# Third and fourth part of a paired feed-forward block exchanged (6, 6, 4, 6), with later activation, rounding and one later product

## The chip, the cores and the metric

The kernel runs on one core of a Trainium2 chip. The metric is the device time of one execution in microseconds (us); the kernel before takes 2537.56 us, the median of 3 runs (2536.77 to 2540.05). The core has a matrix engine (TensorE, PE in the profile), a vector engine (VectorE, DVE), an activation engine (ScalarE, ACT), a general engine (GpSimd, POOL) and SyncE (SP), which here only issues transfers. Each works through a queue of its own in order.

## The reference

The reference is one step of a streaming encoder of two layers, for 512 prompt frames and 64 sample frames that share one set of weights. All is float32, with a model width of 1024. Cut to what matters:

```python
def swiglu(x, w_gu, w_down):
    gate, up = jnp.split(x @ w_gu, 2, axis=-1)      # w_gu: 1024 x 5632
    return (jax.nn.silu(gate) * up) @ w_down        # w_down: 2816 x 1024

for l in range(2):
    x = x + 0.5 * swiglu(rms_norm(x, ln_ffn1[l]), w_ffn1_gu[l], w_ffn1_down[l])
    x = x + mixer(rms_norm(x, ln_mix[l]))           # l=0: attention heads and a short convolution; l=1: state space
    x = x + cross_attend(rms_norm(x, ln_cross[l]), mem_k, mem_v, w_xq[l], w_xo[l])
    x = x + 0.5 * swiglu(rms_norm(x, ln_ffn2[l]), w_ffn2_gu[l], w_ffn2_down[l])
y = rms_norm(x, ln_final)
```

The outputs are y for both groups of frames and the new caches of the mixers and of the memory attention. Of the four feed-forward blocks (FFNs) the change touches three: the second of layer 0 and both of layer 1.

## The kernel before, in words

**Layout.** The 512 + 64 frames lie side by side as 576 columns, in two halves of 288; features lie on the 128 partitions. The state X is 8 tiles of 128 features, and the hidden layer of an FFN has 2816 features, 22 tiles. Every float32 product is made of three products of rounded operands: a weight is split into a rounded part `wh` (by ACT, `hi`, L148) and a rest `wl` (by DVE, `lo`, L154; in steps that are not paired L231), an input likewise into `xh` and `xl` (hidden tiles into `hh`, `hl`), and PE adds wh·xh, wh·xl and wl·xh.

**Pairs.** In the three FFNs of the list `LAYERS_S` the gate and up tile of one hidden tile (called gate/up pair gN here, N from 0 to 21), and each two output tiles f and f + 4 of the down projection (down pair d0 to d3), are computed together in the manner of Strassen and Winograd: seven products over half the rows and half the columns of the operands, in place of eight, with sums of weights and differences of inputs as operands (`eh`, `el` are rounded differences of the normed input; `qeh`, `qel` those of the hidden tiles). g2.3 is product k = 3 of gate/up pair 2. A gate/up product has 12 matmuls (4 tiles of 128 rows by 3 parts), a down product as many tiles as the hidden part has halved: 3 tiles and 9 matmuls for a part of 6 hidden tiles. The matmuls of all pair products stand in one line, L340.

**Banks.** A pair has three PSUM banks, called T, Y and W (`PLACE`): products 0, 3, 4 and 6 write T in turn, 1 and 5 write Y, 2 writes W. Pairs take two sets of banks alternately. After each product an epilogue reads the bank: `pair_epi` (L555) for gate/up, with the evictions L570 (ACT, `tb`), L572 (DVE, `ta` = T + tb), L578 (ACT, `tc`) and L600 (DVE, `tc` = T + tb), the multiplication by the norm's factor (L585), the silu (L588), and after the pair's last product the hidden tile (L618 to L620) and its differences `hk` (L624, or L627 to L629). Then `tail` asks ACT for their rounding and `rest` asks DVE for the rests. `down_epi` (L648) adds a product to X (L655).

**Order of products.** `pair_steps` (L316) gives product k of pair n the place 7n + at[k] from tables written by hand, sorts the products by place, and issues them as steps. `at` has entries of its own for the first two pairs, for the last pair and for d0. `defer(fn, n)` (L399) holds a request back for n further steps; `tick` counts them.

**Weights.** `run_steps` (L166) runs ahead of the product that PE is at: SP loads both tiles of a pair (L292, L293; at most three loads open, at most some eleven products ahead), POOL issues an accumulating transfer into the second buffer (L301), DVE makes the sum `ss` (L310) when the pair's product 2 is prepared, and POOL accumulates twice into the first buffer (L312, L314). Rounding by ACT and DVE is done a few products ahead of the matmuls.

**Parts.** The hidden tiles are worked in parts, `PARTS_S` = 6, 6, 6 and 4 tiles. After the gate/up pairs of a part, and the first one of the next, come the part's four down pairs; their products overlap the neighbours'. The last part's down projection is not paired ("direct"): for each of 8 output tiles, 3 matmuls per hidden tile and column half. For the first two FFNs that is `down` (matmuls in `proj`, L419; X at L727), for the last `down_two` and `down_final` with 320 and then 256 columns (matmuls L738, X at L743), followed by the final norm and its transposes (L2230, L2232). Columns of the down weights are laid out by `KORDER`, so that in a paired part the even hidden tiles come ahead of the odd ones.

Of the kernel before, what the change touches and what calls it, by code (L numbers as in the profile page):

```python
# [22 lines left out]
FF = 2816  # L23
NJ = 22
PARTS = ((0, 6), (6, 8), (14, 8))
PARTS_S = ((0, 6), (6, 6), (12, 6), (18, 4))
KORDER = [j0 + j for j0 in (0, 6, 12) for j in (0, 2, 4, 1, 3, 5)] + [18, 19, 20, 21]
LAYERS_S = ((2, 0), (1, 1), (2, 1))
PAIRED = (0, 4, 1, 5, 2, 6, 3, 7)
PAST = 256  # L30
# [55 lines left out]
class Kernel:  # L86
# [229 lines left out]
    def pair_steps(self, pairs):  # L316

        mm = self.nc.tensor.matmul  # L320
        todo = []
        for n, pr in enumerate(pairs):
            pr.banks = [self.banks[:, 3 * (n % 2) + b, :HF] for b in range(3)]
            at = {2: 0, 0: 3, 1: 4, 3: 6, 5: 8, 4: 9, 6: 12}
            if n < 2:
                at = ({0: 0, 1: 1, 2: 4, 3: 6, 5: 8, 4: 9, 6: 12}, {0: -5, 1: -4, 2: -2, 3: 0, 4: 3, 5: 4, 6: 7.5})[n]
            elif n == len(pairs) - 1:
                at = {0: 0, 2: 0.5, 3: 3, 1: 4, 4: 6, 5: 7, 6: 9}
            elif pr.f == 0:
                at = {0: 0, 2: 3, 1: 4, 3: 6, 5: 8, 4: 9, 6: 12}  # L330
            todo += [(7 * n + at[k], k, pr) for k in range(7)]

        def one(w, k, pr):
            out = pr.banks[PLACE[k]]
            xh, xl = pr.ops()[k]
            kn = pr.kw // 128
            for kk in range(kn):
                ws = slice(kk * 128, kk * 128 + 128)
                for pi, (ww, xx) in enumerate(((w[0], xh), (w[0], xl), (w[1], xh))):
                    mm(out, ww[:, ws], xx[:, kk], start=k < 3 and kk == 0 and pi == 0, stop=kk == kn - 1 and pi == 2,  # L340
                       skip_group_check=True)
            pr.epi(k, pr)

        for _, k, pr in sorted(todo, key=lambda t: t[0]):
            self.step(lambda w, k=k, pr=pr: one(w, k, pr), Part(pr, k))
# [204 lines left out]
    def ffn(self, gu, dn, gain_next, pairs=True, early=False):  # L550
# [1 line left out]
        V = nc.vector  # L552
        st = {}

        def pair_epi(k, pr, first, last, direct):  # L555

            T, Y, W = pr.banks
            tt = V.tensor_tensor
            jj = pr.jj
# [15 lines left out]
            elif k == 1:  # L575
                self.hi(pr.tb[:, two], Y)
            elif k == 3:
                self.hi(pr.tc[:, one], T)  # L578
                if first:
                    st["r"] = self.stats_tok(self.acc, self.ones, 1.0, ps=self.banks[:, 6:8])  # L580
                elif "R" not in st:
                    st["dg"] = self.diag(st["r"], "td")
            elif k == 5:
                def gate(c=slice(0, NT)):
                    tt(pr.ta[:, c], pr.ta[:, c], st["R"][:, c], op=ALU.mult)  # L585

                def silu():
                    nc.scalar.activation(pr.ta, pr.ta, AF.Silu)  # L588

                tt(pr.ta[:, two], Y, pr.tc[:, one], op=ALU.add)  # L590
                if first:
                    st["R"] = self.stats_bcast(None, dg=st.pop("dg"), ps=self.banks[:, 6:8])
                if last:
                    gate(two)
                    silu()
                else:
                    gate()
                    self.defer(silu, 1)
            elif k == 4:
                tt(pr.tc[:, two], T, pr.tb[:, two], op=ALU.add)  # L600
            else:
                qh, ql = st["qhh"], st["qhl"]
                kk = jj // 2
                hk = st["hk"]
                if direct or jj % 2:
                    h = self.tmp("td")
                else:
                    h = hk[:, 1:3].rearrange("p c n -> p (c n)")
                if last:
                    hh, hl = st["hh"][:, jj], st["hl"][:, jj]  # L610
                    for c, x in ((one, T), (two, pr.tc[:, two])):
                        tt(h[:, c], x, pr.ta[:, c], op=ALU.mult)
                        tt(h[:, c], h[:, c], st["R"][:, c], op=ALU.mult)
                        self.hi(hh[:, c], h[:, c])
                    for c in (one, two):
                        self.lo(hl[:, c], h[:, c], hh[:, c])
                    return
                tt(h[:, one], T, pr.ta[:, one], op=ALU.mult)  # L618
                tt(h[:, two], pr.tc[:, two], pr.ta[:, two], op=ALU.mult)
                tt(h, h, st["R"], op=ALU.mult)  # L620
                if direct:
                    parts = [(st["hh"][:, jj], st["hl"][:, jj], h)]
                elif jj % 2 == 0:
                    tt(hk[:, 0], hk[:, 1], hk[:, 2], op=ALU.subtract)  # L624
                    parts = [(qh[:, 0:2, kk], ql[:, 0:2, kk], hk[:, 0:2])]
                else:
                    tt(hk[:, 2], h[:, two], hk[:, 2], op=ALU.subtract)  # L627
                    V.scalar_tensor_tensor(hk[:, 1], hk[:, 2], -1.0, hk[:, 1], op0=ALU.mult, op1=ALU.subtract)
                    V.scalar_tensor_tensor(hk[:, 0], h[:, one], -1.0, hk[:, 1], op0=ALU.mult, op1=ALU.subtract)  # L629
                    parts = [(qh[:, 2:4, kk], ql[:, 2:4, kk], self.h2(h)),  # L630
                             (st["qeh"][:, :, kk], st["qel"][:, :, kk], hk[:, 1:3]),
                             (qh[:, 4, kk], ql[:, 4, kk], hk[:, 0])]

                def rest():
                    for oh, ol, x in parts:
                        self.lo(ol, x, oh)

                def tail():
                    for oh, ol, x in parts:
                        self.hi(oh, x)  # L640
                    self.defer(rest, 0 if first or jj == 5 else 1)

                if jj == 0 and not first:
                    st["held"] = tail
                else:
                    self.defer(tail, 0 if first or jj == 5 else 1)

        def down_epi(k, pr, last):  # L648

# [9 lines left out]
        ops = lambda: self.pair_ops(self.xh, self.xl, self.eh, self.el)  # L659
# [3 lines left out]

        def gate_up(j, jj, nj, direct):
            pr = Pair(gu[2 * j], gu[2 * j + 1],
                      lambda k, pr: pair_epi(k, pr, j == 0, direct and jj == nj - 1, direct), ops)
            pr.jj, pr.begun = jj, False
            seq.append(pr)

# [4 lines left out]

        parts = PARTS_S if pairs else PARTS
        for pi, (j0, nj) in enumerate(parts):
# [97 lines left out]
            for jj in range(0 if pairs else nj):  # L774
                j = j0 + jj
# [1581 lines left out]
def host_arrays(i):  # L2357
# [23 lines left out]
    for n in ("1", "2"):  # L2381
        out["gu" + n] = gu(f(f"w_ffn{n}_gu"))
        out["dn" + n] = np.stack([cols(w) for w in f(f"w_ffn{n}_down")])
        for l in range(2):
            if (int(n), l) in LAYERS_S:
                w = out["dn" + n][l].reshape(8, 128, NJ, 128)
                out["dn" + n][l] = w[:, :, KORDER].reshape(8, 128, NJ * 128)

# [84 lines left out]
```

## Time and profile before

| what | before |
|---|---|
| time, median of 3 runs | 2537.56 us |
| profiled execution | 2532.74 us |
| its span | 2531.0 us |
| mean granted TensorE clock | 0.989 |
| busy PE / DVE / ACT / POOL | 2445.7 / 1841.0 / 1154.5 / 619.1 us |
| paired FFNs, about | 917 to 1328, 1328 to 1733, 2116 to 2531 us |

The profile is one execution, with times from the start of its span. Rows of the timeline and of a tile or line give start, duration, engine, line, operation, output and inputs, shape, and in brackets how long the engine was idle ahead of it and what released it. A group's row gives count, then busy us and the mean in ns, then the idle time. Rows of the waits give the total, the number and the longest. The chain of waits, or chain that ended last, gives start, length, and what ran. The granted clock is a share of TensorE's full speed.

### The profile page before, as it was taken

The numbers are of one execution on the slowest core, as the hardware profiler recorded it, in microseconds if no ns is written. First come the engines' busy times: TensorE is split into PE (matmuls) and PEld (weight loads), VectorE is DVE, ScalarE is ACT, GpSimd is POOL, SyncE is SP. The second block draws the span as 40 slices with busy tenths as digits, with TensorE's granted clock in tenths as the row PEclk, the third lists the DMA queues.
The fourth block names the chain that finished last, engine by engine and source line by source line (L and its number), as shares of the span: only waits on it lengthen the run. The fifth ranks groups of instructions, "written<-read, shape, count | busy, mean of one in ns | idle before, by whom it ended". The sixth has DMA issues, their size and how long they took to land.

```text
span 2531.0 us, 46506 instructions
## 1 busy us (share of the span) xinstructions
PE 2445.7 (97%) x18175; PEld 2398.4 (95%) x18175; DVE 1841.0 (73%) x3350; ACT 1154.5 (46%) x2099; POOL 619.1 (24%) x775
## 2 busy tenths in 40 slices
PE   8999999999999999999989999999999999999997
PEld 8999999999899999999979999999999999999997
DVE  5645658667875588898888888876743468888885
ACT  5222222324664455445455454453443455554544
POOL 1576235202420012222202222212311001222221
PEclk9999999999999999999999999999999999999998
DMA  4365653321134355767736767665972235576771
GB/s 149 92 187 185 155 127 114 127 87 36 41 124 134 106 134 129 181 155 161 154 101 142 165 144 175 141 166 191 297 242 83 77 101 134 134 179 152 160 156 63
DMA packets 160091, 353.21 MB, mean 140 GB/s; under 512 B 21584, under 2 KB 64256, under 8 KB 159232
## 3 DMA queue, kind: packets, MB, share of 16 engines
q1 hardware_dynamic: 115808, 277.09, 34.1%
q0 software_dynamic: 44064, 73.16, 18.7%
q8 instruction: 143, 2.34, 0.4%
q14 instruction: 76, 0.62, 0.1%
HBM read 293.83 MB, written 31.97 MB: 129 GB/s over the span
## 4 chain that ended last, share of the span: by engine, by line
PE 63%; DVE 20%; ACT 6%; DMA 4%; issue 4%; POOL 3%; SPq 0%; DVEq 0%; ACTq 0%; POOLq 0%
PE banks L340 26%; PE banks L419 25%; DVE wl L154 3%; ACT wh L148 2%; PE banks L1988 2%; DVE wl L231 2%; PE banks L2264 2%; PE banks L1884 1%; DVE hl L154 1%; PE banks L1369 1%; PE banks L1337 1%; DMA b<-in_ssm_bw 1%; DVE td L620 1%; ACT hh L148 1%; DMA s5y<-yw 1%
## 5 line engine op out<-in xcount | busy, mean ns | idle before, releaser
L148 ACT ACTIVATE wh<-wraw 128x512 fp32r<-128x512 f32 (+3 forms) x639 | 441.6, 713 | 290.6 <-PE banks L340 104.6
L231 DVE TENSOR_TENSOR wl<-wraw,wh 128x1024 fp32r<-128x1024 f32 (+2 forms) x216 | 260.3, 1209 | 146.7 <-ACT wh L148 144.2
L340 PE MATMUL banks<-xh,wh 128*128 128x288 f32 x1056 | 314.1, 297 | 3.1 <-ACT wh L148 1.9
L340 PE MATMUL banks<-xh,wl 128*128 128x288 f32 x1056 | 314.0, 297 | 1.8 <-DVE wl L154 1.8
L340 PE MATMUL banks<-xl,wh 128*128 128x288 f32 x1056 | 314.0, 297 | 0.2 <-DVE xl L156 0.2
L154 DVE TENSOR_TENSOR wl<-wraw,wh 128x512 fp32r<-128x512 f32 (+1 forms) x408 | 259.3, 640 | 62.8 <-ACT wh L148 60.8
L419 PE MATMUL banks<-xh,wh 128*128 128x288 f32 x1232 | 268.6, 300 | 9.5 <-ACT wh L148 8.6
L419 PE MATMUL banks<-xh,wl 128*128 128x288 f32 x1232 | 266.4, 298 | 3.2 <-DVE wl L231 3.2
L419 PE MATMUL banks<-xl,wh 128*128 128x288 f32 x1232 | 266.0, 298 | 0.0
L340 PE MATMUL banks<-eh,wh 128*128 128x288 f32 x792 | 239.2, 302 | 26.9 <-DVE tc L600 14.5
L340 PE MATMUL banks<-el,wh 128*128 128x288 f32 x792 | 235.5, 297 | 0.0
L340 PE MATMUL banks<-eh,wl 128*128 128x288 f32 x792 | 235.4, 297 | 0.0
L314 POOL DMA_DIRECT2D wraw<-ss x102 | 89.4, 884 | 537.4 <-DVE ta L572 215.9
L419 PE MATMUL banks<-hh,wh 128*128 128x288 f32 x968 | 209.2, 298 | 4.6 <-ACT wh L148 2.0
L419 PE MATMUL banks<-hl,wh 128*128 128x288 f32 x968 | 208.5, 297 | 4.7 <-DVE hl L154 4.7
L419 PE MATMUL banks<-hh,wl 128*128 128x288 f32 x968 | 208.3, 297 | 3.4 <-DVE wl L231 3.2
L419 PEld LDWEIGHTS banks<-xh,wh 128*128 128x128 f32 x1232 | 200.0, 190 | 11.8 <-ACT wh L148 9.1
L340 PEld LDWEIGHTS banks<-xh,wh 128*128 128x128 f32 x1056 | 201.1, 190 | 3.8 <-ACT wh L148 2.3
L419 PEld LDWEIGHTS banks<-xh,wl 128*128 128x128 f32 x1232 | 200.4, 191 | 4.6 <-DVE wl L231 4.4
L340 PEld LDWEIGHTS banks<-xh,wl 128*128 128x128 f32 x1056 | 200.6, 190 | 2.3 <-DVE wl L154 2.3
L340 PEld LDWEIGHTS banks<-xl,wh 128*128 128x128 f32 x1056 | 200.8, 190 | 0.4 <-DVE xl L156 0.4
L419 PEld LDWEIGHTS banks<-xl,wh 128*128 128x128 f32 x1232 | 200.6, 191 | 0.0
(564 smaller groups left out, 6307.1 us busy)
## 6 DMA issues: line engine op xcount, KB each, us to landing
wraw<-in_gu SPq DMA_DIRECT2D x110, 512.0 KB
raw<-in_gu SPq DMA_DIRECT2D x66, 512.0 KB
wraw<-in_dn SPq DMA_DIRECT2D x44, 384.0 KB
raw<-in_gu POOLq DMA_DIRECT2D x66, 256.0 KB, 6.1
wraw<-in_gu POOLq DMA_DIRECT2D x66, 256.0 KB, 4.4
wraw<-ss POOLq DMA_DIRECT2D x66, 256.0 KB, 3.9
raw<-in_dn SPq DMA_DIRECT2D x36, 384.0 KB
wraw<-in_win SPq DMA_DIRECT2D x17, 512.0 KB
```

The lines of the kernel that those rows point to most:

```text
L148: self.nc.scalar.activation(out, in_, AF.Copy)
L154: self.nc.vector.tensor_tensor(out, in_, hi.bitcast(F32), op=ALU.subtract)
L231: self.lo_engine.tensor_tensor(l[:p, :n], t[:p, :n], h[:p, :n].bitcast(F32), op=ALU.subtract)
L314: self.nc.gpsimd.dma_start(pr.r1[:, two], pr.src[3], accum_op=ALU.add)
L340: mm(out, ww[:, ws], xx[:, kk], start=k < 3 and kk == 0 and pi == 0, stop=kk == kn - 1 and pi == 2, skip_group_check=True)
L419: mm(ps[:M, h, :n], ww[:, k * M:(k + 1) * M], xx[:, k0 + k, h * n:(h + 1) * n], start=first and k == 0 and pi == 0, stop=last and k == kt ...
L620: tt(h, h, st["R"], op=ALU.mult)
L1337: mm(out, x[:, k, t * 128:t * 128 + m], y[:, k], start=k == 0 and pi == 0, stop=k == 1 and pi == 2)
L1369: mm(out, x[:, k, f * 128:(f + 1) * 128], y[:, k, ts], start=k == 0 and pi == 0, stop=k == 1 and pi == 2)
L1884: mm(pv[:, m], x[:, kk, ms], y[:, k * MEM:(k + 1) * MEM], start=kk == m == pi == 0, stop=kk == 7 and pi == 2 and m == 1)
L1988: mm(ps[:, h, :HF], ww[:, k * 128:(k + 1) * 128], xx[:, k, h * HF:(h + 1) * HF], start=k == 0 and pi == 0, stop=k == 7 and pi == 2)
L2264: self.nc.tensor.matmul(out, ww[:, k * 128:(k + 1) * 128], xx[:, k], start=k == 0 and pi == 0, stop=k == KT - 1 and pi == 2)
```

## The change

The parts become 6, 6, 4 and 6 tiles, and `KORDER` follows. In the second pair's table the last product goes from place 7.5 to 10.5, which sets g1.6 behind g2.0 instead of ahead of it. The silu is held back for two steps instead of one. The rounding (`tail`) is held back for one step everywhere; before, it was asked for in the same step in the FFN's first pair and in pairs with `jj` = 5. The rest (`rest`) comes in the same step as that in the first pair and in the last pair of any part (`early`). The number of seven-product pairs, 22 gate/up and 12 down in each FFN, stays.

```diff
--- before.py
+++ after.py
@@ -23,8 +23,8 @@
 FF = 2816
 NJ = 22
 PARTS = ((0, 6), (6, 8), (14, 8))
-PARTS_S = ((0, 6), (6, 6), (12, 6), (18, 4))
-KORDER = [j0 + j for j0 in (0, 6, 12) for j in (0, 2, 4, 1, 3, 5)] + [18, 19, 20, 21]
+PARTS_S = ((0, 6), (6, 6), (12, 4), (16, 6))
+KORDER = [j0 + j for j0, n in PARTS_S[:-1] for e in range(2) for j in range(e, n, 2)] + list(range(16, NJ))
 LAYERS_S = ((2, 0), (1, 1), (2, 1))
 PAIRED = (0, 4, 1, 5, 2, 6, 3, 7)
 PAST = 256
@@ -323,7 +323,7 @@
             pr.banks = [self.banks[:, 3 * (n % 2) + b, :HF] for b in range(3)]
             at = {2: 0, 0: 3, 1: 4, 3: 6, 5: 8, 4: 9, 6: 12}
             if n < 2:
-                at = ({0: 0, 1: 1, 2: 4, 3: 6, 5: 8, 4: 9, 6: 12}, {0: -5, 1: -4, 2: -2, 3: 0, 4: 3, 5: 4, 6: 7.5})[n]
+                at = ({0: 0, 1: 1, 2: 4, 3: 6, 5: 8, 4: 9, 6: 12}, {0: -5, 1: -4, 2: -2, 3: 0, 4: 3, 5: 4, 6: 10.5})[n]
             elif n == len(pairs) - 1:
                 at = {0: 0, 2: 0.5, 3: 3, 1: 4, 4: 6, 5: 7, 6: 9}
             elif pr.f == 0:
@@ -552,7 +552,7 @@
         V = nc.vector
         st = {}
 
-        def pair_epi(k, pr, first, last, direct):
+        def pair_epi(k, pr, first, last, direct, early):
 
             T, Y, W = pr.banks
             tt = V.tensor_tensor
@@ -595,7 +595,7 @@
                     silu()
                 else:
                     gate()
-                    self.defer(silu, 1)
+                    self.defer(silu, 2)
             elif k == 4:
                 tt(pr.tc[:, two], T, pr.tb[:, two], op=ALU.add)
             else:
@@ -638,12 +638,12 @@
                 def tail():
                     for oh, ol, x in parts:
                         self.hi(oh, x)
-                    self.defer(rest, 0 if first or jj == 5 else 1)
+                    self.defer(rest, 0 if early else 1)
 
                 if jj == 0 and not first:
                     st["held"] = tail
                 else:
-                    self.defer(tail, 0 if first or jj == 5 else 1)
+                    self.defer(tail, 1)
 
         def down_epi(k, pr, last):
 
@@ -663,7 +663,7 @@
 
         def gate_up(j, jj, nj, direct):
             pr = Pair(gu[2 * j], gu[2 * j + 1],
-                      lambda k, pr: pair_epi(k, pr, j == 0, direct and jj == nj - 1, direct), ops)
+                      lambda k, pr: pair_epi(k, pr, j == 0, direct and jj == nj - 1, direct, j == 0 or jj == nj - 1), ops)
             pr.jj, pr.begun = jj, False
             seq.append(pr)
```

The opening of the first of the three paired FFNs, on DVE: `L618` to `L629` are the epilogue of the second pair's last product, `L572` the eviction of bank T after the third pair's product 0. Before:

```order
1008 L154 TENSOR_TENSOR wl<-ss,wh 128x512
1009 L154 TENSOR_TENSOR hl<-hk,hh 128x2x288
1010 L154 TENSOR_TENSOR wl<-wraw,wh 128x512
1011 L310 TENSOR_TENSOR ss<-raw_10116,wraw 128x512
1012 L618 TENSOR_TENSOR td<-banks,ta 128x288
1013 L619 TENSOR_TENSOR td<-tc,ta 128x288
1014 L620 TENSOR_TENSOR td<-td,R 128x576
1015 L627 TENSOR_TENSOR hk<-td,hk 128x288
1016 L628 SCALAR_TENSOR_TENSOR hk<-hk 128x288
1017 L629 SCALAR_TENSOR_TENSOR hk<-td,hk 128x288
1018 L154 TENSOR_TENSOR wl<-wraw,wh 128x512
1019 L572 TENSOR_TENSOR ta<-banks,tb 128x288
```

After:

```order
1008 L154 TENSOR_TENSOR wl<-ss,wh 128x512
1009 L154 TENSOR_TENSOR wl<-wraw,wh 128x512
1010 L310 TENSOR_TENSOR ss<-raw_10116,wraw 128x512
1011 L572 TENSOR_TENSOR ta<-banks,tb 128x288
1012 L154 TENSOR_TENSOR hl<-hk,hh 128x2x288
1013 L154 TENSOR_TENSOR wl<-wraw,wh 128x512
1014 L618 TENSOR_TENSOR td<-banks,ta 128x288
1015 L619 TENSOR_TENSOR td<-tc,ta 128x288
1016 L620 TENSOR_TENSOR td<-td,R 128x576
1017 L627 TENSOR_TENSOR hk<-td,hk 128x288
```

`L572` went from the twelfth place to the fourth and now stands ahead of `L618`; the rest of the first hidden differences (`hl`) stands behind it.

The same place on ACT, where `L588` is the silu, `hh<-hk` the rounding of hidden differences, `tb<-banks` an eviction and the others are roundings of weights. Before:

```order
485 L148 ACTIVATE wh<-raw_9669 128x512
486 L148 ACTIVATE wh<-wraw 128x512
487 L148 ACTIVATE wh<-raw_9810 128x512
488 L588 ACTIVATE ta<-ta 128x576
489 L148 ACTIVATE hh<-hk 128x2x288
490 L148 ACTIVATE wh<-ss 128x512
491 L148 ACTIVATE tb<-banks 128x288
```

After:

```order
485 L148 ACTIVATE wh<-raw_9669 128x512
486 L148 ACTIVATE wh<-raw_9810 128x512
487 L148 ACTIVATE wh<-ss 128x512
488 L148 ACTIVATE tb<-banks 128x288
489 L588 ACTIVATE ta<-ta 128x576
490 L148 ACTIVATE hh<-hk 128x2x288
491 L148 ACTIVATE wh<-wraw 128x512 x3
```

The rounding of the sum `ss` and the eviction went ahead of the silu and of `hh`.

The end of the first part on ACT, where the first down products begin; weights of 128x384 belong to down products, `tc<-banks` is the eviction ahead of `L600`. Before:

```order
540 L148 ACTIVATE wh<-wraw 128x512
541 L148 ACTIVATE hh<-td 128x2x288
542 L148 ACTIVATE qeh<-hk 128x2x288
543 L148 ACTIVATE hh<-hk 128x288
544 L148 ACTIVATE wh<-wraw 128x384
545 L148 ACTIVATE tc<-banks 128x288
546 L148 ACTIVATE wh<-raw_10610 128x384
```

After:

```order
541 L148 ACTIVATE wh<-wraw 128x512
542 L148 ACTIVATE wh<-wraw 128x384
543 L148 ACTIVATE tc<-banks 128x288
544 L148 ACTIVATE hh<-td 128x2x288
545 L148 ACTIVATE qeh<-hk 128x2x288
546 L148 ACTIVATE hh<-hk 128x288
547 L148 ACTIVATE wh<-raw_10610 128x384
```

One weight rounding and the eviction went ahead of the three roundings of hidden differences.

The third part's down products on DVE, at the sum `ss` (`L310`) for the next gate/up pair; `L655` adds a product to X, roundings of 128x384 or 128x256 belong to down products. Before:

```order
1484 L154 TENSOR_TENSOR wl<-ss,wh 128x384
1485 L655 SCALAR_TENSOR_TENSOR X<-banks,X 128x288
1486 L154 TENSOR_TENSOR wl<-wraw,wh 128x512
1487 L310 TENSOR_TENSOR ss<-raw_13504,wraw 128x512
1488 L655 SCALAR_TENSOR_TENSOR X<-banks,X 128x288
1489 L154 TENSOR_TENSOR wl<-wraw,wh 128x384
1490 L655 SCALAR_TENSOR_TENSOR X<-banks,X 128x288
```

After:

```order
1448 L154 TENSOR_TENSOR wl<-ss,wh 128x256
1449 L655 SCALAR_TENSOR_TENSOR X<-banks,X 128x288
1450 L154 TENSOR_TENSOR wl<-wraw,wh 128x512
1451 L310 TENSOR_TENSOR ss<-raw_13199,wraw 128x512
1452 L655 SCALAR_TENSOR_TENSOR X<-banks,X 128x288
1453 L154 TENSOR_TENSOR wl<-wraw,wh 128x256
1454 L655 SCALAR_TENSOR_TENSOR X<-banks,X 128x288
```

The place of the sum among the products is the same; the down weights' roundings are narrower.

## The prediction

> **What bounds the kernel now.** I read the page first: the shares of the engines and the granted clock.
>
> ```profile
> span 2531.0 us, 46506 instructions
> PE 2445.7 (97%) x18175; PEld 2398.4 (95%) x18175; DVE 1841.0 (73%) x3350; ACT 1154.5 (46%) x2099; POOL 619.1 (24%) x775
> ```
>
> TensorE (PE) is busy 97% of 2531.0 us. So time is gained in two ways: fewer matmuls, or fewer of the stretches in which PE stands or runs at a lower clock. The windows of the three paired FFNs come next (length; busy us of PE, PEld, DVE, ACT, POOL; granted clock; DMA share; GB/s). The first row is the pair stage of the first paired FFN, the others are the direct down stages of the three.
>
> ```profile
> 917.00:1285.00 368.00, 356.70 (x2645) 353.11 (x2643) 312.14 (x607) 189.97 (x375) 86.88 (x99) 0.99 0.67 149
> 1285.00:1328.00 43.00, 34.81 (x228) 32.03 (x228) 37.51 (x65) 24.87 (x47) 3.48 (x4) 0.96 0.44 117
> 1683.00:1733.00 50.00, 46.16 (x344) 45.26 (x342) 35.32 (x62) 26.04 (x43) 12.26 (x11) 1.00 0.48 166
> 2476.00:2531.00 55.00, 41.64 (x282) 39.87 (x280) 29.36 (x78) 22.21 (x51) 9.64 (x12) 0.84 0.21 67
> ```
>
> In the pair stage PE is the bound and DVE stands close behind it (312 of 368 us). In the first direct stage DVE is busier than PE (37.5 against 34.8 us): matmuls added there are partly free. In the second PE leads, so they are not. In the third nothing is near its limit and the clock is 0.84.
>
> The waits, totalled over the run (us, times, longest), show what stops PE in the pair stage.
>
> ```profile
> PE banks L340 <- DVE tc L600: 14.5, 24, 1.3
> PE banks L340 <- ACT wh L148: 13.7, 5, 3.9
> PE banks L738 <- DVE hl L154: 2.9, 1, 2.9
> PE banks L2230 <- ACT fy L2232: 2.0, 1, 2.0
> ```
>
> The second row holds one stall near each paired FFN's opening, three of 3.9 us; the first is a short one at every change from gate/up to down products. For costs I take the spacing of matmuls from the chain that ended last: 40.80/306 = 0.133 us at 288 columns; in the last direct stage 1.76/12 = 0.147 (320 columns) and 1.43/12 = 0.119 (256).
>
> ```profile
> 1015.13 40.80 PE banks L340 x306
> 2501.24 1.76 PE banks L738 x12
> 2518.32 1.43 PE banks L738 x12
> ```
>
> **The change part by part.** All sums are changes against the profiled execution, 2532.74 us (span 2531.0), which lies 4.8 below the median of 2537.56; I apply the same difference to the median.
>
> *First: the opening of each FFN.* The timeline around the stall (start, duration):
>
> ```profile
> 947.24 0.29 PE L340 MATMUL banks<-xh,wl 128*128 128x288 f32 x1
> 951.46 0.58 PE L340 MATMUL banks<-eh,wh 128*128 128x288 f32 x1 [3.93 <-ACT wh L148]
> 947.25 0.45 DVE L618 TENSOR_TENSOR td<-banks,ta 128x288 f32<-128x288 f32 x1
> 949.88 0.46 DVE L629 SCALAR_TENSOR_TENSOR hk<-td,hk 128x288 f32<-128x288 f32 x1
> 950.86 0.45 DVE L572 TENSOR_TENSOR ta<-banks,tb 128x288 f32<-128x288 f32 x1
> 951.40:957.40 6.00, 5.94 (x25) 5.97 (x26) 3.78 (x6) 1.76 (x5) 0.88 (x1) 0.51 0.76 168
> ```
>
> PE has nothing from 947.24 until 951.46. The view names ACT, whose last rounding ended about then too; but product g2.3 writes bank T, and T is read until 951.31 by DVE's L572, which stands in its queue behind the second pair's whole epilogue (L618 at 947.25 to L629 at 949.88, six operations). The change puts g1.6 one product later, so this epilogue is asked for later, and L572 comes ahead of L618. ACT's three roundings likewise no longer stand behind L588 and hh. The stall is 951.46 − 947.24 = 4.22 less one spacing 0.133, 4.09 us. After it the clock was 0.51 for 6 us: 25 matmuls, which at 0.133 take 3.35, so 2.65 lost. Together 6.7 us. Following the new order with the durations above, I am left with about 0.45 us at g2.4, which waits for the reading of T, and 0.9 at g2.6, one eviction behind two others. So −5.4 per FFN, **−16.2** for three; bounds −20 (nothing left) and −8 (half of it comes back at these two places).
>
> *Second: parts of 6, 6, 4, 6.* The number of products is the same, but a down product of the third part has 2 tiles of 128 instead of 3: 4 pairs × 7 products × 3 = 84 matmuls fewer, 84 × 0.133 = −11.2 us per FFN. The direct stage has 6 tiles instead of 4: 8 outputs × 2 more tiles × 3 matmuls × 2 halves = 96 more. What they cost differs by FFN.
>
> ```profile
> 1285.72 0.53 PE L419 MATMUL banks<-hl,wh 128*128 128x288 f32 x2 [2.10 <-DVE hl L154]
> 2483.89 0.64 PE L738 MATMUL banks<-hl,wh 128*128 128x320 f32 x1 [2.94 <-DVE hl L154]
> 2483.90:2489.80 5.90, 5.90 (x22) 5.90 (x23) 2.19 (x5) 0.90 (x3) 0.00 (x0) 0.50 0.18 47
> L231 DVE TENSOR_TENSOR wl<-wraw,wh 128x512 fp32r<-128x512 f32 x38 | 27.9, 739 | 14.2 <-ACT wh L148 12.5 <-POOL pb L1092 1.6
> L231 DVE TENSOR_TENSOR wl<-wraw,wh 128x768 fp32r<-128x768 f32 x8 | 8.0, 1005 | 1.8 <-ACT wh L148 1.8
> ```
>
> In the first direct stage DVE sets the pace: each of its weight roundings goes from 512 to 768 columns, 739 to 1005 ns, five of them in the stage's path, 1.3 us, and 0.3 for the rest: +1.6. In the second PE sets it: 96 × 0.133 = 12.75; the added tiles also give PE work while the last hidden tile is rounded (the wait for hl, 2.10 in the row), which I take as saving 1.7: +11.0. In the last, 48 × 0.147 + 48 × 0.119 = 12.8. Of it comes back: 1.0 of the wait of 2.94; the half clock after it (22 matmuls in 5.9 us at 0.50, where 3.3 would do), 2.6; the wait of 2.0 for fy with its slow matmuls and idle PE in a first pass that DVE paces, 4.5 as I judge from PE's 41.6 of 55 us: +4.7. Second part in sum: 3 × −11.2 + 1.6 + 11.0 + 4.7 = **−16.3**; bounds −8 (nothing comes back in the last stage, and 12.8 is paid) and −20 (half of the second stage's hides too).
>
> *Third: activation and rounding a step later, at the boundaries.* PE, then DVE, where the first part's down products begin, and last a silu from the opening:
>
> ```profile
> 1009.25 0.37 PE L340 MATMUL banks<-eh,wh 128*128 128x288 f32 x1 [1.28 <-DVE tc L600]
> 1003.41 0.56 DVE L154 TENSOR_TENSOR wl<-wraw,wh 128x384 fp32r<-128x384 f32 x1 [1.01 <-ACT wh L148]
> 1008.66 0.45 DVE L600 TENSOR_TENSOR tc<-banks,tb 128x288 f32<-128x288 f32 x1
> 940.91 0.69 ACT L588 ACTIVATE ta<-ta 128x576 f32<-128x576 f32 x1 [0.74 <-DVE ta L585]
> ```
>
> g6.6 waits 1.28 us for L600, which is late because DVE itself stood 1.01 at 1003.41 for a weight rounding that ACT had behind three hidden-tile roundings. The change sets that weight rounding ahead of them. DVE's idle 1.01 goes, but the rounded differences then come later and fill part of it, so I credit PE with 0.45 at each of 9 boundaries: **−4**; bounds 0 and −9. The silu asked for a step later itself costs nothing: it has the steps until the pair's last product, and that cover is at least one product of 12 × 0.133 = 1.6 us; without it the silu's 0.69 us would be on the path once a pair. The last pair of the last part rounds at once in a branch of its own, which the change leaves.
>
> *Fourth: what the shorter products uncover in the third part.* The load of a pair's weights goes SP, then an accumulating transfer from POOL (L301), then DVE's sum (L310). Before, around the end of the third part's down products:
>
> ```profile
> 1223.08 0.33 SPq L293 DMA_DIRECT2D raw<-in_dn  x1
> 1232.64 0.56 DVE L310 TENSOR_TENSOR ss<-raw,wraw 128x384 f32<-128x384 f32 x1
> 1230.29 0.33 SPq L293 DMA_DIRECT2D raw<-in_gu  x1
> 1235.23 0.86 POOL L301 DMA_DIRECT2D raw<-in_gu  x1 [0.50 <-DMA raw<-in_gu]
> 1241.38 0.69 DVE L310 TENSOR_TENSOR ss<-raw,wraw 128x512 f32<-128x512 f32 x1
> 1648.06 0.69 DVE L310 TENSOR_TENSOR ss<-raw,wraw 128x512 f32<-128x512 f32 x1 [1.14 <-DMA raw<-in_gu]
> 1228.00:1236.00 8.00, 8.00 (x62) 8.00 (x62) 6.81 (x15) 3.76 (x8) 2.78 (x4) 1.00 0.85 205
> L655 DVE SCALAR_TENSOR_TENSOR X<-banks,X 128x288 f32<-128x288 f32 x22 | 10.0, 456 | 2.2 <-PE banks L340 2.1
> L154 DVE TENSOR_TENSOR wl<-wraw,wh 128x384 fp32r<-128x384 f32 x12 | 6.6, 553 | 1.1 <-ACT wh L148 1.1
> L154 DVE TENSOR_TENSOR wl<-wraw,wh 128x512 fp32r<-128x512 f32 x2 | 1.4, 688 | 0.1
> ```
>
> From SP's issue to the sum it takes 1232.64 − 1223.08 = 9.6 us for a down pair and 1241.38 − 1230.29 = 11.1 for the next gate/up pair. SP's issue and the sum are tied to places in the order of products. A down product of three tiles takes 9 × 0.133 = 1.2 us, so 11.1 us are 9.25 products; of two tiles they are 9.25 × 0.8 = 7.4 us. The chain has no slack to give: in the second FFN the same sum already waits 1.14 us for its transfer. So g17's sum should come 3.7 us late, less a little slack that the first FFN shows: 3.4. Behind it in DVE's queue stands L655 of d3.0, the eviction of the bank that d3.3 writes: PE stands about 3.4 us there. The sum of d3 is late in the same way, by 9.6 × (1 − 0.67) = 3.2 less what the smaller transfer and the earlier gate/up products give back, 1.5 us on PE; and DVE has no room to catch up: a rounding of 256 columns is 0.42 us (553 ns at 384, 688 at 512, so 0.135 less) and an L655 0.456, 0.87 in a step of 0.8, so that I count 0.8 more at the start, where the pair's sums come on top. 5.7 to 6.0 per FFN, **+17.5**; bounds 0 (the transfers come as much sooner as the steps are shorter) and +25.
>
> Does the clock fall after these stalls? It fell to half after 3.93 us and after 2.94 us of idle PE; 2.10 us before 1285.72 left it up (the clock in that window is 0.96). A stall of 3.4 lies beyond 2.94 but may be split by late matmuls; a fall costs 2.6. I count it once: **+2.6**; bounds 0 and +7.8. [...]
>
> Sum: −16.2 − 16.3 − 4 + 17.5 + 2.6 = **−16.4**, so 2516.3 for a profiled execution and **2521** for the median.
>
> **The rivals.**
> *A, no new wait in the third part.* If the loads are issued early enough that the sums never wait, 2.4 us (0.8 three times) remain of the fourth term and no clock falls: −16.2 − 16.3 − 4 + 2.4 = −34.1, 2503. For it: three buffers and DMA engines that are not full (share 0.67 to 0.85). Against it: the sum that waits 1.14 us before the steps are shortened.
> *B, the opening's stall is only moved.* If g2.4 and g2.6 take what g2.3 lost and the clock falls as before, the gain there shrinks from 16.2 to some 6 (half the wait): −6, 2531. For it: DVE still has the same six epilogue operations to do in these microseconds. Against it: they then stand behind all evictions that PE needs next.
> *C, slower.* In the third part the pairs' weights come one pair at a time: the chain of 9.6 us then sets a down pair where 7 × 1.2 = 8.4 us of matmuls did. The 84 matmuls save nothing, and each of 4 pairs takes 1.2 us more, 14.4 for three FFNs. With the direct stages' +17.3, the opening and the boundaries: 14.4 + 17.3 − 16.2 − 4 = +11.5, 2549. It loses against the kernel before from the point where a down pair of the third part takes over 8.6 us. For it: the 9.6 and 11.1 us. Against it: in the window 1228 to 1236 PE was never idle at 8.4 us a pair, so loads of two pairs overlap.
> *D, the change doesn't do what it says*: the order of products and of ACT's roundings shows that the moves take place, so I leave it only a part of B.
>
> **How the numbers follow.** Forecast 0.50, A 0.25, B 0.15, C 0.06, the rest 0.04 between. The forecast's own range from the bounds of its terms, not all at one end, is 2510 to 2533. The range must leave out at most 2 in 10: from 2500, which holds A with 3 us of room, to 2536, which holds B. A measurement of this kernel can tell about 0.2%, 5.1 us: faster is below 2532.5 and slower above 2542.6. Faster: 0.92 of the forecast, all of A, 0.75 of B, 0.82. Slower: C and a little of the rest, 0.07. The remaining 0.11 is no change.
>
> **What would show it.** In the changed profile: L572 of the third pair ahead of L618 of the second, no idle over 1 us before g2.3, and a clock near 1.0 there, in all three FFNs; if an idle of 3 us or more stands at g2.4 or g2.6 instead, B is right. The pair stage of 368 us shorter by 9 to 15. An L310 that waits 3 us for its transfer, with an idle PE behind it, at the last of the third part's down products; if L310 waits under 1 us there, A is right; if it waits in every down pair, C. The direct stages longer by 1.6, 11 and 5 us, without the half clock at the start of the last. My forecast is wrong in its core if PE's idle time in the third part stays what it was, or if the direct stage of the first FFN grows by more than 5 us.

## The result, and the profile after

The changed kernel takes 2522.59 us (median of 4 runs, 2519.18 to 2525.58), the kernel before beside it 2537.16 us. The ratio is 0.9943, with a 95% interval of 0.9924 to 0.9963: 9 to 19 us faster, 14.6 by the medians, where 16.4 was forecast. A second measurement with five rounds gave 0.9954 (0.9942 to 0.9966). The profiled execution, 2525.58 us, was the slowest of the four, so the two traces differ by 7.3 us only. I use them for places, and the ratios for sizes. All ratios are of fast runs; of the parts alone, below, one of eight executions took 6050 us and is left out.

The page and the waits of PE, to be set beside those of before:

```profile
span 2523.7 us, 46551 instructions
PE 2444.6 (97%) x18211; PEld 2399.9 (95%) x18211; DVE 1818.1 (72%) x3332; ACT 1152.7 (46%) x2093; POOL 619.9 (25%) x775
PE banks L340 <- DVE tc L600: 11.5, 21, 1.2
PE banks L340 <- DVE X L655: 8.7, 5, 3.7
PE banks L340 <- ACT ta L588: 5.9, 3, 2.0
PE banks L340 <- ACT wh L148: 4.9, 3, 2.5
PE banks L738 <- DVE hl L154: 3.0, 1, 3.0
```

There are 36 matmuls more (12 per FFN: 84 fewer, 96 more). The three stalls of 3.9 us are gone. L655 now costs 8.7 us, with one wait of 3.7; in the kernel before it had no wait over 0.7:

```profile
PE banks L340 <- DVE X L655: 3.8, 8, 0.7
```

The row of the silu, L588, is new, and the wait of 3 us for hl in the last stage is there as before.

The same four windows, cut where the work begins and ends now, and the opening:

```profile
919.00:1276.00 357.00, 346.11 (x2574) 342.62 (x2572) 302.83 (x599) 186.37 (x371) 87.08 (x99) 1.00 0.67 150
1276.00:1326.00 50.00, 46.33 (x343) 45.43 (x342) 42.42 (x71) 28.86 (x51) 6.16 (x7) 1.00 0.45 115
1670.00:1725.00 55.00, 52.58 (x393) 51.89 (x391) 32.03 (x52) 25.69 (x39) 11.63 (x11) 1.00 0.44 147
2462.00:2523.70 61.70, 50.03 (x362) 49.17 (x360) 29.83 (x75) 22.93 (x50) 9.69 (x12) 0.91 0.20 65
951.40:957.40 6.00, 5.63 (x43) 5.40 (x42) 5.26 (x10) 4.91 (x10) 0.88 (x1) 1.00 0.74 161
```

The window after g2.3 held 25 matmuls at a clock of 0.51 before and holds 43 at 1.00 now. A sum over the whole run follows from the starts of the first and last matmul of line L340 in each FFN (here those of the first FFN after the change):

```profile
919.87 0.29 PE L340 MATMUL banks<-xh,wh 128*128 128x288 f32 x1
1272.53 0.30 PE L340 MATMUL banks<-eh,wl 128*128 128x288 f32 x1
```

| stretch | before, us | after, us | difference |
|---|---|---|---|
| pair stage of the three FFNs | 363.7, 372.4, 363.6 | 352.7, 357.5, 352.4 | −11.1, −14.9, −11.2 |
| from its end to the next FFN's first pair product | 33.5, 428.6 | 40.2, 440.8 | +6.8, +12.2 |
| from the last one's end to the end of the run | 51.3 | 60.2 | +8.9 |

With 2.2 us at the start, in code that the change doesn't touch, these make the 7.3 us. The second gap also holds two stages that the change leaves alone. Over the profiles of all kernels below it is 438.7 us in five with the new parts and 430.3 in four with the old (all before the last edit below), so 8.4 is a better value than 12.2.

### The profile page after: what moved, and what is told of

It reads as the page before. It is cut to its first block, busy times and chain, and to the rows that moved or that the text cites. A ratio compares the mean times of both kernels' runs of the same rounds, so it can differ in the third digit from the quotient of the medians.

```text
span 2523.7 us, 46551 instructions
## 1 busy us (share of the span) xinstructions
PE 2444.6 (97%) x18211; PEld 2399.9 (95%) x18211; DVE 1818.1 (72%) x3332; ACT 1152.7 (46%) x2093; POOL 619.9 (25%) x775
## 4 chain that ended last, share of the span: by engine, by line
PE 62%; DVE 19%; DMA 6%; ACT 6%; issue 4%; POOL 3%; SPq 1%; DVEq 0%; ACTq 0%; POOLq 0%
PE banks L419 26%; PE banks L340 24%; DVE wl L154 3%; ACT wh L148 2%; PE banks L1988 2%; DVE wl L231 2%; DVE hl L154 2%; PE banks L738 1%; PE banks L1369 1%; PE banks L1337 1%; PE banks L2264 1%; DMA raw<-in_gu 1%; DMA b<-in_ssm_bw 1%; DVE td L620 1%; DMA f<-s5f 1%
## 5 line engine op out<-in xcount | busy, mean ns | idle before, releaser
L148 ACT ACTIVATE wh<-wraw 128x512 fp32r<-128x512 f32 (+4 forms) x639 | 446.3, 714 | 346.2 <-PE banks L340 127.1
L340 PE MATMUL banks<-xh,wh 128*128 128x288 f32 x1056 | 312.1, 296 | 1.3 <-ACT wh L148 1.3
L340 PE MATMUL banks<-xh,wl 128*128 128x288 f32 x1056 | 312.1, 296 | 0.9 <-DVE wl L154 0.9
L340 PE MATMUL banks<-xl,wh 128*128 128x288 f32 x1056 | 312.0, 295 | 0.0
L154 DVE TENSOR_TENSOR wl<-wraw,wh 128x512 fp32r<-128x512 f32 (+2 forms) x408 | 252.6, 623 | 46.1 <-ACT wh L148 45.1
L340 PE MATMUL banks<-eh,wh 128*128 128x288 f32 x792 | 236.7, 299 | 18.5 <-DVE tc L600 11.5
L340 PE MATMUL banks<-el,wh 128*128 128x288 f32 x792 | 234.2, 296 | 0.0
L340 PE MATMUL banks<-eh,wl 128*128 128x288 f32 x792 | 234.1, 296 | 0.0
L419 PE MATMUL banks<-hl,wh 128*128 128x288 f32 x1032 | 222.7, 298 | 3.4 <-DVE hl L154 3.4
L419 PE MATMUL banks<-hh,wh 128*128 128x288 f32 x1032 | 223.0, 298 | 2.6 <-ACT hh L148 1.8
L419 PE MATMUL banks<-hh,wl 128*128 128x288 f32 x1032 | 222.4, 297 | 2.7 <-DVE wl L231 2.7
L340 PEld LDWEIGHTS banks<-xh,wh 128*128 128x128 f32 x1056 | 199.4, 189 | 1.7 <-ACT wh L148 1.5
L340 PEld LDWEIGHTS banks<-xh,wl 128*128 128x128 f32 x1056 | 199.0, 188 | 1.1 <-DVE wl L154 1.1
L340 PEld LDWEIGHTS banks<-xl,wh 128*128 128x128 f32 x1056 | 199.1, 189 | 0.0
```

The costliest lines, as they stand in the source:

```text
L148: self.nc.scalar.activation(out, in_, AF.Copy)
L154: self.nc.vector.tensor_tensor(out, in_, hi.bitcast(F32), op=ALU.subtract)
L419: mm(ps[:M, h, :n], ww[:, k * M:(k + 1) * M], xx[:, k0 + k, h * n:(h + 1) * n], start=first and k == 0 and pi == 0, stop=last and k == kt ...
```

## The experiments

Below, a product's *loss* is the time between the first matmuls of two products that follow each other, less 0.133 us for each matmul of the first.

**The parts alone, and everything but the parts.** Two kernels split the change:

```diff
# parts_only: the kernel before with
-PARTS_S = ((0, 6), (6, 6), (12, 6), (18, 4))
+PARTS_S = ((0, 6), (6, 6), (12, 4), (16, 6))   # and KORDER
# all_but_parts: the changed kernel with the old PARTS_S and KORDER
```

> The changed kernel once more, as the yardstick of the three beside it. Both theories: 12 to 17 us below the kernel before.

> The kernel before with the parts 6, 6, 4, 6 alone; opening and roundings as before. Theory (the parts cost what they save): 33.6 us of matmuls saved, about 20 lost again in the third part and 20 in the direct stages, so 2 to 10 us slower than before (ratio 1.001 to 1.004), and the opening stall of 4.1 us still there three times. Rival (the exchange of parts carries the gain): 8 us or more faster than before (ratio under 0.997).

> The changed kernel with the parts 6, 6, 6, 4 of before; the later product, silu and rounding stay. Theory: the whole gain is in these, 18 to 24 us below before (ratio 0.990 to 0.993), 4 to 10 us below the changed kernel. Rival (the exchange of parts carries the gain): under 10 us below before, and slower than the changed kernel.

Measured on one chip: the changed kernel 0.9954 (0.9942 to 0.9966), the parts alone 1.0026 (1.0015 to 1.0037), all but the parts 0.9922 (0.9909 to 0.9936). In microseconds of a kernel of 2532.6: −11.7, +6.6 and −19.8. The exchange of parts is a loss of 7 to 8 us by itself; the later product, silu and rounding bring all of the gain, and more. The forecast had said −20.2 for these and +3.8 for the parts with their stalls. In the trace of the parts alone the three stalls of 3.9 us are still there (first row), and L655 has grown from 3.8 us to 13.7:

```profile
PE banks L340 <- ACT wh L148: 14.0, 6, 3.9
PE banks L340 <- DVE X L655: 13.7, 15, 2.3
```

**The opening: the later product, or the later rounding?** The profile had named ACT's weight rounding as what released g2.3, and the prediction had named DVE's L572. One kernel moves L572 and leaves the silu and the roundings of hidden tiles asked for as before, the other does the opposite:

```diff
# table_only: the kernel before with
-{0: -5, 1: -4, 2: -2, 3: 0, 4: 3, 5: 4, 6: 7.5}
+{0: -5, 1: -4, 2: -2, 3: 0, 4: 3, 5: 4, 6: 10.5}
# later_only: all_but_parts with this table as before
```

> The kernel before with the second pair's last product at 10.5 in place of 7.5, and nothing else. On DVE the eviction L572 goes ahead of the second pair's epilogue; on ACT the silu and the rounding of hidden differences still stand ahead of the third pair's weight rounding. Theory (DVE's queue holds bank T): the stall before g2.3 falls from 4.1 us to under 1.5, no half clock, 8 to 14 us below the kernel before. Rival (ACT's late weight rounding, which the profile names): about 4 us stay at g2.3 and less than 4 us are gained.

> The kernel before with the silu and the rounding a step later, the table of products and the parts as before. On ACT the weight rounding goes ahead of silu and hidden differences; on DVE L572 still stands behind the second pair's epilogue. Theory: g2.3 still waits 2 to 4 us for L572, the boundaries gain some 0.7 us nine times, 5 to 11 us below the kernel before. Rival (ACT): the stall at g2.3 goes, 15 us or more below.

The later product alone gave 0.9945 (0.9932 to 0.9959), −13.9 us; the later roundings alone 0.9966 (0.9955 to 0.9978), −8.6. Their sum, −22.5, differs from the −19.8 of both together by less than the intervals, so it is not shown that the two overlap. In the second kernel part of the computation is changed: the rest of the first pair's hidden differences is taken after g1.6's epilogue has written over them, so what it computes is wrong. The operations and their shapes are the same, and in both traces L572 takes 0.45 us and a weight rounding of 128x512 0.61, so its times can be compared with those of the kernel before. It shows why the table and the delays belong together: a rounding that is asked for later needs the next pair's epilogue later too.

First the later product alone, g2.3 and, on DVE and ACT, what stands around it:

```profile
949.66 0.37 PE L340 MATMUL banks<-eh,wh 128*128 128x288 f32 x1 [0.33 <-DVE ta L572]
946.58 0.69 DVE L154 TENSOR_TENSOR wl<-ss,wh 128x512 fp32r<-128x512 f32 x1 [1.27 <-ACT wh L148]
949.07 0.45 DVE L572 TENSOR_TENSOR ta<-banks,tb 128x288 f32<-128x288 f32 x1
945.94 0.61 ACT L148 ACTIVATE wh<-ss 128x512 fp32r<-128x512 f32 x1
```

ACT's rounding is as late as before and DVE idles the same 1.27 us for it, yet PE stands 0.33 us in place of 3.93. Then the later roundings alone:

```profile
955.80 0.58 PE L340 MATMUL banks<-eh,wh 128*128 128x288 f32 x1 [3.97 <-ACT wh L148]
950.80 0.45 DVE L618 TENSOR_TENSOR td<-banks,ta 128x288 f32<-128x288 f32 x1
955.20 0.45 DVE L572 TENSOR_TENSOR ta<-banks,tb 128x288 f32<-128x288 f32 x1
```

ACT's order is the new one, the profile names ACT again, and the stall is 3.97 us: L572 still comes 4.4 us after L618 and ends at 955.65, 0.15 ahead of the matmul. One thing the pair of kernels leaves open. The weight rounding that ended just ahead of the stall's end, at 950.81 in the kernel before, is not held fixed by them: in the first kernel it too goes ahead of the second pair's hidden roundings, and in the second it stays behind them. What settles it is which rounding g2.3 reads. Product 3 takes the sum `ss`; counted in the order of products, the rounding at 950.81 belongs to g2.4. In the kernel before (first two rows) and in the second kernel (last row):

```profile
944.13 0.61 ACT L148 ACTIVATE wh<-ss 128x512 fp32r<-128x512 f32 x1
950.81 0.61 ACT L148 ACTIVATE wh<-wraw 128x512 fp32r<-128x512 f32 x1
944.38 0.61 ACT L148 ACTIVATE wh<-ss 128x512 fp32r<-128x512 f32 x1
```

The rounding that g2.3 needs was done 6.7 us ahead of its matmul at 951.46, and 10.8 us ahead in the second kernel. So it was DVE's queue. What the second kernel gains in its trace is at the boundaries: 1.44 us became 1.30 at g6.6, 0.23 went at g6.4, and 0.62 became 0.2 at d0.4.

**The third part: loads that start too late?** A down pair of 4 tiles needs 512 columns for each of its two weights, where a load buffer has 1024. The edit puts both into one buffer, so that more pairs fit, and widens two windows while such a pair is open (cut to what matters):

```diff
-if self.fs is None or st["open"] >= 3 or i > st["prepped"] + 11:
+w, r = g.pair.use = use(g.pair)      # (1, 1); a 4-tile down pair (1, 0) or (0, 1)
+if self.fs is None or w and st["open"] >= 3 or r and st["raw"] >= 3 or i > st["prepped"] + far(g.pair):
...
-while st["summed"] < min(st["issued"], st["prepped"] + 5):
+while st["summed"] < min(st["issued"], st["prepped"] + (8 if st["small"] else 5)):
...
+pr.r1, pr.r2 = (w, r) if w is not None and r is not None else ((w, r)[w is None][:, c:c + n] for c in (0, n))
# far: 18 while a 4-tile pair is open, else 11; lead_buf keeps 11 and 5
```

> The changed kernel with loads of the third part issued earlier: a down pair of 4 tiles needs 512 columns for each of its two weights, so both share one load buffer, up to six pairs may be open instead of three, and the windows of loads and of accumulating transfers reach 18 and 8 products ahead instead of 11 and 5 there. Theory (the chain from load to sum starts too late for products of 0.8 us): no sum waits over 1 us in the third part, and 12 to 20 us below the changed kernel. Rival (the accumulating transfers are slow by the traffic itself, or POOL's order holds them): the sums still wait 2 to 3 us, and less than 4 us are gained.

> The kernel with earlier loads, but with the windows of 11 and 5 products as before: only the shared load buffers stay. Theory (a load starts when a buffer comes free): within 4 us of the kernel with both, 2500 to 2506. Rival (the windows in products set the start, and products have become shorter): under 6 us below the changed kernel, and the sums of the third part wait again.

Earlier loads: 2501.47 us, 0.9882 (0.9866 to 0.9898), beside 0.9954 of the changed kernel on the same chip, some 18 us. The buffers alone: 0.9901 (0.9888 to 0.9914), 4.8 us by the ratios behind the kernel with both, where at most 4 were expected, and 13 ahead of the changed kernel; so most of the gain is theirs. The intervals of the two overlap, so what the windows add is not shown. Where the changed kernel stood in the second FFN:

```profile
1607.63 0.69 DVE L310 TENSOR_TENSOR ss<-raw,wraw 128x512 f32<-128x512 f32 x1 [3.37 <-DMA raw<-in_gu]
1608.24 0.45 DVE L655 SCALAR_TENSOR_TENSOR X<-banks,X 128x288 f32<-128x288 f32 x1
1608.83 0.58 PE L340 MATMUL banks<-qeh,wh 128*128 128x288 f32 x1 [3.71 <-DVE X L655]
```

That is the chain of the prediction: the sum waits for its transfer, L655 stands behind it, and d3.3 for the bank. With the earlier loads, DVE's waits in the first FFN's third part (1180 to 1216) are these; none is for a transfer:

```profile
DVE wl L154 <- ACT wh L148: 2.6, 3, 1.5
DVE td L633 <- PE banks L355: 0.3, 1, 0.3
DVE X L670 <- PE banks L355: 0.2, 1, 0.2
```

(Lines after the edit are some 15 higher: L355 is L340.) So the rival A could be had, but by an edit of its own.

**The direct stage: what does its first wait hang on?** The added tiles should have covered the wait for hl in the last stage, and did not. The operation that PE waits for is the rest of the *last but one* hidden tile, which `defer` puts behind the last pair's epilogue. On the kernel with earlier loads:

```diff
-direct, j == 0 or jj == nj - 1), ops)
+direct, j == 0 or jj == nj - 1 or direct and jj == nj - 2), ops)
```

> The kernel with earlier loads, and in the direct part the rest of the last but one hidden tile asked for in the same step as its rounding; on DVE that one operation goes from behind the last pair's epilogue to ahead of it, three times. Theory (the direct stages wait for this rest, not for weights or for PE's order): the wait of 3.0 us for hl in the last direct stage falls below 1.5 and the half clock behind it goes, 1 to 2 us in each of the other two; 5 to 9 us below the kernel with earlier loads. Rival (the wait is for the last tile, whose chain is as long as before): the wait stays within 0.5 us of 3.0 and nothing is gained.

> The kernel with earlier loads and early rest once more, on the same chip as the next one. If the silu's delay is worth what the traces show at the starts of the down products (d0.4, 0.4 us at nine places and 1 to 3 us elsewhere), this one is 4 to 8 us faster than the next; if it is worth nothing, the two agree within 3 us.

It gave 2494.37 us, 0.984 (0.9824 to 0.9857), and on another chip 2497.24 us, 0.9865 (0.9847 to 0.9883): the fastest kernel of this study, 1.4 to 1.6% below the one before. Against 0.9882 that is 4 to 11 us; the traces account for about 6: 1.6 us in the first direct stage, 2.8 in the last, and the second taken like the first. Before this edit, in the changed kernel, and with it:

```profile
2466.92 1.72 DVE L154 TENSOR_TENSOR hl<-td,hh 128x288 fp32r<-128x288 f32 x3
2468.69 0.64 PE L738 MATMUL banks<-hl,wh 128*128 128x320 f32 x1 [3.00 <-DVE hl L154]
2468.70:2474.70 6.00, 6.00 (x22) 6.00 (x23) 1.07 (x2) 0.00 (x0) 0.00 (x0) 0.50 0.24 67
```

```profile
2437.36 0.75 DVE L154 TENSOR_TENSOR hl<-td,hh 128x576 fp32r<-128x576 f32 x1
2438.19 0.46 DVE L627 TENSOR_TENSOR td<-banks,ta 128x288 f32<-128x288 f32 x1
2435.00:2442.00 7.00, 7.00 (x51) 7.00 (x50) 5.77 (x11) 2.90 (x5) 0.00 (x0) 1.00 0.21 63
```

One operation of 0.75 us moved into a gap in which DVE waited for the silu anyway (0.76 us in the changed kernel), and PE stands no more.

**Which parts, once the waits are gone?** The same edit with the old parts:

> The changed kernel with parts 6, 6, 6, 4, and the rest of the last but one hidden tile asked for at once. It asks which parts are the better ones once each has its own waits removed. Theory (a shorter third part saves matmuls that the direct stage pays back in part): 6 to 11 us below the same parts without this edit, so 24 to 31 us below before (ratio 0.988 to 0.9905), and 8 to 16 us above the kernel with earlier loads and this rest. Rival (the parts are worth nothing either way): within 4 us of that kernel, 38 us or more below before.

2500.59 us, 0.988 (0.9863 to 0.9896): 31 us below the kernel before, at the edge of what was expected. With the new parts and earlier loads the same edit stands at 0.984 and 0.9865, each on another chip, 4 to 10 us better where 8 to 16 were expected, and in the second case the intervals overlap. Without this edit the two were measured on one chip, and there the difference is clear of noise: 0.9882 (0.9866 to 0.9898) with the new parts and earlier loads, 0.9922 (0.9909 to 0.9936) with the old parts, 10 us. So the exchange, a loss of 7 us as it came, is worth some 4 to 10 us when its loads start early enough.

**The silu's delay.**

```diff
-self.defer(silu, 2)
+self.defer(silu, 1)
```

> The kernel with earlier loads and early rest, with the silu held back for one step as before the change. Theory (the silu's own delay costs and brings nothing, since it has several steps of cover): within 4 us of the kernel with two steps (39 to 43 us below before, ratio 0.9825 to 0.9855), the boundary waits for L600 within 0.2 us of those. Rival (the delay is what frees ACT at the boundaries): the boundary waits go back to 1.44 us and a few tenths more, 5 us or more slower.

> The silu held back for one step, as in the run before, beside the kernel with two steps: 4 to 8 us slower than it if the delay is worth something, within 3 us if not.

First 0.9872 (0.9858 to 0.9887), on one chip beside another kernel, then 0.9871 (0.9851 to 0.9891) beside 0.9865 with two steps. Side by side the difference is 4 us by the medians and lies within the intervals. The first expectation, 39 to 43 us below before, was missed (32); the second left it between its two cases. The trace shows one thing clearly: the wait for g6.6 stays at 1.30, so that is the rounding's doing, but d0.4 of the first two parts loses 0.62 again in place of 0.2, and d0.4 of the third 0.69 in place of 0.28 in two of the three FFNs. The delay is worth 0.4 us at each of these places, and if it is worth more, these runs cannot tell.

## Why the prediction was right, point by point

**The opening** (−16.2). Right in place, and nearly in size: −5.3, −4.0 and −5.2 in the traces, −14.6 in sum. The loss around g2.3 went from 6.8 us in the first FFN to the two leftovers that were foreseen, 0.53 at g2.4 (0.45 foreseen) and 0.91 at g2.6 (0.9). By itself the later product measured −13.9. That the named releaser was not the real one is shown by the pair of kernels above and by the rounding that g2.3 reads.

**Parts: matmuls** (−33.6 of pair stages). 2520 matmuls of L340 stand in each FFN in place of 2604. The pair stages became 11.1, 14.9 and 11.2 us shorter, where 9 to 15 was named.

**Parts: direct stages** (+1.6, +11.0, +4.7). The first gap grew by 6.8. That is more than the 5 us which the forecast named as a sign of being wrong in its core; but the next FFN's opening, whose products begin later, loses 6.0 us in place of 10.9, so 4.9 come back there, which the forecast did not separate. Both together are +1.9, close to the forecast. The second, +8.4 over the profiles, was somewhat smaller. The third was the step that failed: +8.9. I had counted that 1.0 us of the wait for hl and 2.6 us of half clock would come back. But PE goes through the first output's tiles in order: of the 12 matmuls added in the first two outputs only 6 stand ahead of the wait (13 in place of 7, 0.9 us), and the chain of ACT and DVE in front of it grew by as much, as its weight roundings are wider (0.69 to 0.96 us on DVE, 0.61 to 0.83 on ACT, two each). The wait stayed, 3.00 us. The half clock stayed too in this profile, 22 matmuls in 6.0 us; in the second profile of the same kernel it is absent, 41 matmuls in 6.0 us at the same place, and the stage is +6.1. By difference, 3.9 of the 12.8 us of matmuls came back in this stage, near the 4.5 counted for the fy wait and the idle first pass; the wait for fy itself fell from 2.0 to 0.6.

**Boundaries** (−4, 0.45 at nine). At the first two of each FFN the losses of 1.44, 0.62 and 0.23 became 1.30, 0.2 and none: 0.8 at six places, −4.7. At the third the shorter products made it worse, 2.13 in place of 1.44, with PE waiting for a bank by way of the silu (5.9, 3, 2.0 in the waits); with the old parts and the other changes it is 1.29 there. This loss is counted in the next item. That the size fits is luck: the forecast credited all of 0.45 to the weight rounding at g6.6, where 0.14 came, with 0.23 at g6.4; the larger part, 0.4 at d0.4, is the silu's delay, of which it expected neither cost nor gain.

**The third part** (+17.5, and +2.6 for the clock). In the traces the losses from g16.6 to the end of the down products are 6.2, 7.3 and 7.3 us more than before: 20.8, where 20.1 was foreseen. About 7 of it are lost at half clock, which came four times and not once (13 matmuls in 3.0 us in place of 23 behind three of the stalls, 21 in 5.0 us behind the fourth); the waits themselves are some 13, less than the 17.5 of the forecast, so that its sum fits better than its terms. In the first FFN the longer wait was that of d3's sum, 2.68 us, in the second that of g17's, 3.37. That the chain starts too late is shown by the earlier loads.

**The sum.** The terms as measured (−14.6, −33.6, +1.9, +8.4, +8.9, −4.7, +20.8) add up to −12.9, and to −15.7 with the last stage of the second profile, where the two measurements gave −14.6 and −11.7. The errors, up to 4 us each, partly cancel.

**The rivals.** A, no new wait, is refuted for this kernel and was reached by an edit. B, the stall only moved, is refuted by the opening's losses. C, weights one pair at a time, did not come about: each FFN lost some 7 us in its third part, and none lost the 11 us that it saved. D: all moves were made.

## What to carry to other kernels

When a wait has several possible releasers, the profile names the one that ended last by its events; move one of them at a time, and look up which of them the waiting instruction reads (here PE stood 3.97 us with ACT's order moved and 0.33 with L572 moved). When a step is shortened, everything that was issued a fixed number of steps ahead loses lead in proportion: widen the window or the buffers together with the step (here the sum for a gate/up pair at the end of the third part, in the second FFN, waited 1.14 us for its transfer before and 3.37 after). And count work that should cover a wait only as far as it stands ahead of the waiting instruction in its engine's order (here 6 of 12 matmuls, 0.9 us).

## What the runs showed of the hardware

The prediction took the fall of the clock as a matter of the idle time alone, after 2.94 us yes, after 2.10 no. The runs show no such limit: behind idle times of 1.96 to 3.00 us of PE the clock was at half in some cases and at full in others. In the last direct stage 22 matmuls stand in 5.9 us behind 2.94 us in the kernel before, and 22 in 6.0 us behind 3.00 in the changed kernel's first profile (above). In its second profile it is 41 at the same place (first row), and 41 behind 2.99 us in the kernel with earlier loads (the other two):

```profile
2466.90:2472.90 6.00, 6.00 (x41) 6.00 (x42) 2.66 (x6) 1.92 (x4) 0.84 (x1) 1.00 0.23 67
2455.46 0.42 PE L753 MATMUL banks<-hl,wh 128*128 128x320 f32 x1 [2.99 <-DVE hl L154]
2455.50:2461.50 6.00, 6.00 (x41) 6.00 (x42) 2.66 (x6) 1.93 (x4) 0.84 (x1) 1.00 0.24 67
```

Ahead of g16.6 PE stands 1.96 to 1.97 us in each of the changed kernel's three FFNs, and of these three stalls only the third has half clock behind it:

```profile
1189.34 0.37 PE L340 MATMUL banks<-eh,wh 128*128 128x288 f32 x1 [1.96 <-ACT ta L588]
1189.40:1192.40 3.00, 3.00 (x23) 3.00 (x24) 2.97 (x9) 1.16 (x4) 1.77 (x2) 1.00 0.19 30
1584.67 0.37 PE L340 MATMUL banks<-eh,wh 128*128 128x288 f32 x1 [1.97 <-ACT ta L588]
1584.70:1587.70 3.00, 3.00 (x23) 3.00 (x24) 2.96 (x9) 1.18 (x4) 1.77 (x2) 1.00 0.18 28
2379.36 0.58 PE L340 MATMUL banks<-eh,wh 128*128 128x288 f32 x1 [1.97 <-ACT ta L588]
2379.40:2382.40 3.00, 3.00 (x13) 3.00 (x14) 1.89 (x6) 0.45 (x2) 1.77 (x2) 0.50 0.17 27
```

In the same profile the clock is at half behind 2.17 and 2.50 us (first four rows), where in the kernel before it was at full behind 2.10 (last two):

```profile
2403.20 0.56 PE L340 MATMUL banks<-qeh,wh 128*128 128x288 f32 x1 [2.17 <-DVE X L655]
2403.30:2406.30 3.00, 3.00 (x13) 3.00 (x14) 2.55 (x7) 1.57 (x3) 2.04 (x3) 0.50 0.60 94
1205.17 0.58 PE L340 MATMUL banks<-qeh,wh 128*128 128x288 f32 x1 [2.50 <-ACT wh L148]
1205.20:1208.20 3.00, 3.00 (x13) 3.00 (x14) 2.35 (x7) 0.57 (x3) 2.66 (x3) 0.50 0.53 101
1691.61 0.40 PE L419 MATMUL banks<-hl,wh 128*128 128x288 f32 x1 [2.10 <-DVE hl L154]
1691.70:1694.70 3.00, 3.00 (x23) 3.00 (x24) 1.93 (x5) 1.49 (x4) 0.00 (x0) 1.00 0.93 363
```

Behind the four longest stalls of the paired FFNs in these two profiles the clock was at half each time (0.50 to 0.54): 3.93, 3.94 and 3.93 us in the kernel before, with 13 matmuls in the 3.0 us after each, and 3.71 in the changed one, with 21 in 5.0 us. What decides at 1.96 to 3.00 us is not shown. As an estimate, a fall cost 2.8 us in the last direct stage: 19 matmuls fewer in 6.0 us, at 0.147 us each. That may be a part of the several us by which the runs of one kernel differ, which was not tried by itself.
